# Column-tile weight splits traced at the highest priority in a four-mixer decoder layer

## The chip, the cores and the metric

The kernel runs on one core of a Trainium2 chip. A core has five engines with instruction queues of their own: TensorE (PE; its weight loads stand apart as PEld), VectorE (DVE), ScalarE (ACT), GpSimd (POOL) and SyncE (SP), which here only issues DMAs. Each engine takes its instructions in the order in which the built program holds them and waits on semaphores for data of the others. The metric is the time of one execution in microseconds of device time. A median over several runs is compared; 0.2% (2.5 us) is about the smallest difference that can be told from none.

## The reference, cut to what matters

One residual layer on x of 1024 tokens by 1024 channels, in float32. A normalised input goes through one combined projection; its columns feed four token mixers (A gated DeltaNet, B spatial gating, C RWKV-7, D native sparse attention) and the merge gates:

```python
h = rmsnorm(x, norm_gain)
proj = h @ w_in
ys = (gated_deltanet(...), spatial_gating(...), rwkv7_time_mix(...), native_sparse_attention(...))
gates = jnp.split(jax.nn.sigmoid(merge), N_MIXERS, axis=-1)
mixed = gates[0] * (ys[0] @ w_branch[0])
for i in range(1, N_MIXERS):
    mixed = mixed + gates[i] * (ys[i] @ w_branch[i])
return x + mixed @ w_out          # and a final rmsnorm
```

## The kernel before, in words

**Products in two halves.** To keep float32 accuracy each matrix is held as a high part (a rounded copy) and a low part (the remainder): `hh` and `hl` for the input, `wh` and `wl` for weights, and one product is three matmuls, `wh*hh`, `wl*hh` and `wh*hl`.

**Column tiles.** `col_tile` makes 128 columns of the projection for all 1024 tokens. It loads its weights in two halves (`load_w`, SP queue, tile `wt`, 3 buffers), splits each half (`split_w`: a cast on ScalarE makes `wh`, a subtraction on VectorE makes `wl`, 3 buffers each), and runs 48 matmuls of 128x512 (L1017 to L1019): 24 into one PSUM bank for the first 512 tokens, 24 into another for the second. The bank (`st`, 2 of them) is emptied by ScalarE into `stg` and stored to DRAM. With three buffers of `wh` and `wl`, one and a half tiles of split weights fit ahead of TensorE. There are 59 such tiles, 2832 matmuls. Three of the projection's tiles are made apart at the start, while the input is being normalised (L1111).

**The mixers.** `rwkv`, `gdn`, `nsa` and `gmlp` are traced one after the other, and their columns before each. Their work is small matmuls and long chains between TensorE, ScalarE and VectorE: in `rwkv` and `gdn` a triangular inverse of 16 steps on VectorE (`unit_lower_inverse`, L98 and L100), and a state that goes through chunks (L301 to L329, L550 to L578). The 32 column tiles of the merge gates are traced last, after `gmlp`.

**What sets the order.** Tile code is traced into a list of instructions, and at build time a list scheduler lays down the order of each engine: among the instructions that are ready in its own model of the machine, it takes the one with the highest priority, which without further words is the one traced earliest. So the column tiles traced after a mixer are the mixer's filler: their matmuls, casts and subtractions stand wherever the mixer's own instructions leave an engine free in that model. Once built, the order is fixed.

**After the mixers.** The outputs of the mixers are read back (`yr`, 16 loads of 256 KB through 2 buffers, L1230) and split into `yh` and `yl` (L1231, L1232); the pool that holds them opens when `gmlp` has ended. Then come the branch products (L1250 to L1252) and the output projection (L1281 to L1284).

Of the kernel before, what the change touches and what calls it, by code (L numbers as in the profile page):

```python
# [68 lines left out]
def bank(G, name="m", bufs=2):  # L69
    return G.ps.tile([128, 512], F32, name=name, bufs=bufs)  # L70
# [910 lines left out]
def body(tc, xT, x, w, wsm, rw_up, rw_cols, gd_conv, gd_hp, gd_gw, gm_ws, gm_bs, gm_lg, gm_lb,  # L981
# [3 lines left out]
    nc = tc.nc  # L985
    with ExitStack() as ctx:
# [10 lines left out]
        def load_w(src, k0, n):  # L997
            wt = sp.tile([128, 4, 128], F32, name="wt", bufs=3)
            nc.sync.dma_start(wt[:, :, :n], src[:, k0:k0 + 4])
            return wt  # L1000

        def split_w(wt, eng=nc.gpsimd, pool=sp, bufs=3):
            wh = pool.tile([128, 4, 128], F32R, name="wh", bufs=bufs)
            nc.scalar.copy(wh, wt)  # L1004
            wl = pool.tile([128, 4, 128], F32R, name="wl", bufs=bufs)
            eng.tensor_sub(wl, wt, wh.bitcast(F32))  # L1006
            return wh, wl

        def col_tile(c, evac):
            parts = [split_w(load_w(w[c], 4 * kh, 128), nc.vector) for kh in range(2)]  # L1010
            for th in range(2):
                sl = slice(512 * th, 512 * th + 512)
                p = bank(G, "st", 2)
                for k in range(8):
                    wh, wl = parts[k // 4]
                    kk = k % 4
                    nc.tensor.matmul(p, wh[:, kk], hh[:, k, sl], start=(k == 0), stop=False)  # L1017
                    nc.tensor.matmul(p, wl[:, kk], hh[:, k, sl], start=False, stop=False)  # L1018
                    nc.tensor.matmul(p, wh[:, kk], hl[:, k, sl], start=False, stop=(k == 7))  # L1019
                evac(p, sl)  # L1020
# [145 lines left out]
        for i in (0, 1, 4, 5):  # L1166
            col_tile(C_RW + i, park(rwd[i]))
        for i in range(2):
            col_tile(C_RWZ + i, park_silu(Z[2][i]))
# [21 lines left out]
        for i in (2, 3, 0, 1, 4, 5):  # L1191
            col_tile(C_GD + i, park(gdd[i]))
# [174 lines left out]
```

## Time and profile before

| | |
|---|---|
| median of three runs | 1254.97 us (1254.69 to 1255.78) |
| the profiled execution | 1258.43 us, of which 1256.7 us from the first to the last instruction |
| TensorE busy | 1185.8 us (94%) in 6214 matmul records |
| VectorE, ScalarE, GpSimd busy | 849.0 us (68%), 519.6 us (41%), 175.2 us (14%) |
| mean granted TensorE clock | 0.977 of full speed |

A busy time is that of the engine's records put together. Matmul records overlap, since one is issued while the last still drains, so a busy TensorE is not one that issues as fast as it can. A matmul of full float32 (transposes and the mixers' small products) leaves two records, one of the column tiles leaves one. The time outside the span (1.7 us) is not in the trace.

### The profile page before, as it was taken

How to read it: one execution, taken by the hardware profiler on the slowest of the kernel's cores; microseconds unless marked ns; L12 is line 12 of the kernel's file. 1: busy time of each engine (PE TensorE's matmuls, PEld its weight loads, DVE VectorE, ACT ScalarE, POOL GpSimd, SP SyncE). 2: the span in 40 equal slices, each digit the busy share in tenths (PEclk: the TensorE clock that was granted, in tenths of full speed). 3: DMA queues.
4: the chain of work that ended last, by engine and by line, in shares of the span. 5: the costliest groups of instructions: out<-in, count | busy, mean ns of one | idle time of the engine just before them, and what ended most of it. 6: DMA issues, size and time to landing. Idle time of an engine off the chain costs nothing. (4 is left out here: it accounts for less than half of the span.)

```text
span 1256.7 us, 17997 instructions
## 1 busy us (share of the span) xinstructions
PE 1185.8 (94%) x6214; PEld 962.6 (77%) x6214; DVE 849.0 (68%) x2181; ACT 519.6 (41%) x1302; POOL 175.2 (14%) x158
## 2 busy tenths in 40 slices
PE   6999999898999997998999999999999799999997
PEld 6987777786777785776777778787877577888886
DVE  6612697878774677878795579989876833588222
ACT  5422553361433355363533355645555343221212
POOL 4320000000002000010100000000000320576510
PEclk9999999998999998999999999999999999999999
DMA  5222453122211444212322422121114275676323
GB/s 196 101 93 101 134 149 103 45 70 67 98 59 59 112 149 121 98 61 81 115 75 85 162 94 76 64 76 56 59 47 145 100 238 186 214 236 217 110 84 126
DMA packets 113103, 140.09 MB, mean 111 GB/s; under 512 B 36544, under 2 KB 59968, under 8 KB 112884
## 3 DMA queue, kind: packets, MB, share of 16 engines
q1 hardware_dynamic: 95588, 107.22, 27.2%
q10 hardware_dynamic: 17424, 31.73, 6.6%
q8 instruction: 49, 0.80, 0.3%
q14 instruction: 42, 0.34, 0.1%
HBM read 94.78 MB, written 44.12 MB: 111 GB/s over the span
## 5 line engine op out<-in xcount | busy, mean ns | idle before, releaser
L1018 PE MATMUL st<-hh,wl 128*128 128x512 f32 x944 | 384.5, 407 | 9.4 <-DVE wl L1006 9.4
L1017 PE MATMUL st<-hh,wh 128*128 128x512 f32 x944 | 381.9, 406 | 3.2 <-ACT stg L1045 2.0
L1019 PE MATMUL st<-hl,wh 128*128 128x512 f32 x944 | 381.3, 404 | 0.0
L1018 PEld LDWEIGHTS st<-hh,wl 128*128 128x128 f32 x944 | 180.8, 192 | 44.0 <-DVE wl L1006 10.9
L1017 PEld LDWEIGHTS st<-hh,wh 128*128 128x128 f32 x944 | 180.2, 191 | 38.0 <-ACT stg L1045 3.5
L1019 PEld LDWEIGHTS st<-hl,wh 128*128 128x128 f32 x944 | 180.9, 192 | 32.3 <-issue 0.8
L1006 DVE TENSOR_TENSOR wl<-wt,wh 128x512 fp32r<-128x512 f32 x134 | 99.3, 744 | 94.2 <-ACT wh L1004 91.7
L1004 ACT CAST wh<-wt 128x512 fp32r<-128x512 f32 x140 | 86.4, 619 | 80.8 <-PE st L1019 66.5
L1045 ACT ACTIVATE stg<-st 128x512 f32<-128x512 f32 x64 | 38.2, 596 | 77.3 <-PE st L1019 76.9
L98 DVE TENSOR_TENSOR invP<-invX,invL 128x32 f32<-128x32 f32 (+15 forms) x128 | 55.7, 435 | 1.7
L100 DVE TENSOR_REDUCE invX<-invP 128x16 f32<-128x32 f32 (+15 forms) x128 | 54.9, 429 | 1.8
L915 ACT ACTIVATE P<-sc,m 128x512 f32<-128x512 f32 (+3 forms) x80 | 44.7, 564 | 25.3 <-DVE m L913 11.6
L1281 PE MATMUL sc<-woh,hh 128*128 128x512 f32 x128 | 49.8, 389 | 0.0
L1282 PE MATMUL sc<-wol,hh 128*128 128x512 f32 x128 | 49.8, 389 | 0.0
L1287 DVE TENSOR_TENSOR o<-sc,xr 128x512 f32<-128x512 f32 x16 | 11.1, 691 | 56.1 <-PE sc L1284 56.1
L1028 ACT COPY stg<-st 128x512 f32<-128x512 f32 x39 | 23.1, 591 | 61.0 <-PE st L1019 57.6
L1258 POOL TENSOR_TENSOR mx<-mx,stg 128x512 f32<-128x512 f32 x28 | 38.6, 1379 | 47.7 <-DVE stg L1257 46.6
L910 DVE TENSOR_REDUCE m<-sc 128x1 f32<-128x512 f32 (+3 forms) x80 | 40.7, 528 | 0.9 <-PE sc L835 0.3
L1264 ACT CAST hh<-mx 128x512 fp32r<-128x512 f32 x16 | 9.9, 621 | 62.6 <-POOL mx L1258 54.8
L30 POOL IOTA tril<- 128x128 f32 x1 | 0.2, 248 | 237.4 <-PE sc L835 237.4
L588 POOL TENSOR_TENSOR gst<-gst,mhalf 128x8 f32<-128x8 f32 x4 | 6.7, 1678 | 190.6 <-DVE gst L587 190.6
L254 POOL MEMSET sv<- 64x512 f32 x8 | 4.2, 519 | 207.8 <-ACT O L292 165.3
(457 smaller groups left out, 2400.7 us busy)
## 6 DMA issues: line engine op xcount, KB each, us to landing
wt<-in_w_dram SPq DMA_DIRECT2D x124, 256.0 KB, 2.7
gate<-stg ACTq DMA_DIRECT2D x64, 256.0 KB, 2.1
gt<-gate SPq DMA_DIRECT2D x32, 256.0 KB, 3.4
stg<-gate SPq DMA_DIRECT2D x32, 256.0 KB, 3.0
xt<-in_xT_dram SPq DMA_DIRECT2D x8, 512.0 KB, 5.0
wot<-in_wo_dram SPq DMA_DIRECT2D x16, 256.0 KB, 3.7
wt<-in_wb_dram SPq DMA_DIRECT2D x16, 256.0 KB, 3.5
xr<-in_x_dram SPq DMA_DIRECT2D x16, 256.0 KB, 2.5
```

The source lines that it names most:

```text
L98: nc.vector.tensor_mul(prv[:, :, :, :m], X[:, :, None, c:].to_broadcast([128, 8, 2, m]), L[:, None, c:c + 2, c:].to_broadcast([128, 8, 2, m]))
L100: nc.vector.tensor_reduce(X[:, :, c:c + 2], prv[:, :, :, :m], axis=AX.X, op=OP.add)
L910: nc.vector.tensor_reduce(m2[:, h, gi:gi + 1], pz[:, :n], axis=AX.X, op=OP.max, negate=True)
L915: nc.scalar.activation(Pt[gi][:, h, :n], pp[gi][:, :n], AF.Exp, bias=m2[:, h, 0:1], accum_out=ss[:, gi, h:h + 1])
L1004: nc.scalar.copy(wh, wt)
L1006: eng.tensor_sub(wl, wt, wh.bitcast(F32))
L1017: nc.tensor.matmul(p, wh[:, kk], hh[:, k, sl], start=(k == 0), stop=False)
L1018: nc.tensor.matmul(p, wl[:, kk], hh[:, k, sl], start=False, stop=False)
L1019: nc.tensor.matmul(p, wh[:, kk], hl[:, k, sl], start=False, stop=(k == 7))
L1258: (nc.vector if j == 7 else nc.gpsimd).tensor_add(mx, mx, g)
L1281: nc.tensor.matmul(p, mh[:, k, ts], a[:, k], start=(k == 0), stop=False)
L1282: nc.tensor.matmul(p, mh[:, k, ts], b[:, k], start=False, stop=False)
```

## The change

Of a column tile, the two instructions of each weight split are traced inside a block of highest priority. Nothing is computed otherwise, and no instruction, buffer or transfer is added; the load and the 48 matmuls keep the priority of their place. The splits of the three first tiles, of the branch weights and of the output weights stay as they were. Lines behind L1010 move by 4.

```diff
         def col_tile(c, evac):
-            parts = [split_w(load_w(w[c], 4 * kh, 128), nc.vector) for kh in range(2)]
+            parts = []
+            for kh in range(2):
+                wt = load_w(w[c], 4 * kh, 128)
+                with tc.high_priority():
+                    parts.append(split_w(wt, nc.vector))
             for th in range(2):
```

The built order differs on TensorE, VectorE, ScalarE and SP (on POOL it is the same). Three places are shown.

VectorE in `gdn`, the first quarter's inverse (`invP`, `invX`, L98 and L100, with 2 more columns at each step) beside the convolution of a later quarter (`cvt`, L465). Before, late in the inverse:

```order
L465 SCALAR_TENSOR_TENSOR cvt<-graw,cw,cvt 128x256
L100 TENSOR_REDUCE invX<-invP 128x8x2
L1038 SCALAR_TENSOR_TENSOR stg<-stg 128x512
L98 TENSOR_TENSOR invP<-invX,invL 128x16x26
L1038 SCALAR_TENSOR_TENSOR stg<-stg 128x512
L100 TENSOR_REDUCE invX<-invP 128x8x2
L480 SCALAR_TENSOR_TENSOR cvt<-gth,cvt 128x512
L98 TENSOR_TENSOR invP<-invX,invL 128x16x28
L1006 TENSOR_TENSOR wl<-wt,wh 128x512
L100 TENSOR_REDUCE invX<-invP 128x8x2
L1006 TENSOR_TENSOR wl<-wt,wh 128x512
```

Now, in the middle of the same inverse:

```order
L100 TENSOR_REDUCE invX<-invP 128x8x2
L1006 TENSOR_TENSOR wl<-wt,wh 128x512
L98 TENSOR_TENSOR invP<-invX,invL 128x16x12
L465 SCALAR_TENSOR_TENSOR cvt<-graw,cw,cvt 128x256
L100 TENSOR_REDUCE invX<-invP 128x8x2
L465 SCALAR_TENSOR_TENSOR cvt<-graw,cw,cvt 128x256
L98 TENSOR_TENSOR invP<-invX,invL 128x16x14
L465 SCALAR_TENSOR_TENSOR cvt<-graw,cw,cvt 128x256
L100 TENSOR_REDUCE invX<-invP 128x8x2
L1006 TENSOR_TENSOR wl<-wt,wh 128x512
L98 TENSOR_TENSOR invP<-invX,invL 128x16x16
```

Three splits stood together at the inverse's end; five now lie spread over it. By buffer number, the first of the three stood 61 rows behind the start of this inverse (L92) and now stands 10 rows ahead of it.

TensorE in `gdn`, one chunk of the state's chain (L560, L542, L544, L572, L576; rows of L1017 to L1019, now L1021 to L1023, are column tiles). Before:

```order
L576 MATMUL sc<-gSA_3540,gTB 128x128
L1019 MATMUL st<-hl,wh 128x512
L1017 MATMUL st<-hh,wh 128x512
L560 MATMUL sc<-gS,KQ_3536 128x128
L542 MATMUL sc<-gS,KQ_3536 128x128
L544 MATMUL sc<-gSA_3540,gKK 128x128
L572 MATMUL sc<-gR,gXT_3538 128x64
L576 MATMUL sc<-gSA_3539,gTB 128x128
```

Now, from L542 of the same chunk on:

```order
L542 MATMUL sc<-gS,KQ_3536 128x128
L544 MATMUL sc<-gSA_3540,gKK 128x128
L1023 MATMUL st<-hl,wh 128x512
L1021 MATMUL st<-hh,wh 128x512
L1022 MATMUL st<-hh,wl 128x512
L572 MATMUL sc<-gR,gXT_3538 128x64
L1023 MATMUL st<-hl,wh 128x512
L1021 MATMUL st<-hh,wh 128x512
L1022 MATMUL st<-hh,wl 128x512
L1023 MATMUL st<-hl,wh 128x512
L1021 MATMUL st<-hh,wh 128x512
L576 MATMUL sc<-gSA_3539,gTB 128x128
```

Where two column-tile matmuls stood between one L576 and the next, thirteen stand now (five of them ahead of L560).

SP's DMA issues after `gmlp`: loads of mixer outputs (`yr`), of output weights (`wot`), of parked gates (`gt`), and of weights into `wt`, either a column tile's (`in_w_dram`) or a branch product's (`in_wb_dram`). Before:

```order
L1230 DMA yr<-y__101 128x512
L999 DMA wt<-in_w_dram 128x512
L1230 DMA yr<-y__101 128x512
L1217 DMA wot<-in_wo_dram 128x512 x2
L1245 DMA gt<-gate_136 128x512
L1230 DMA yr<-y__101 128x512 x2
L1217 DMA wot<-in_wo_dram 128x512 x2
L999 DMA wt<-in_w_dram 128x512
L1230 DMA yr<-y__104 128x512
```

Now:

```order
L999 DMA wt<-in_wb_dram 128x512 x2
L1234 DMA yr<-y__101 128x512 x2
L1221 DMA wot<-in_wo_dram 128x512 x2
L1249 DMA gt<-gate_120 128x512
L1234 DMA yr<-y__101 128x512 x2
L1221 DMA wot<-in_wo_dram 128x512 x2
L999 DMA wt<-in_wb_dram 128x512
L1234 DMA yr<-y__104 128x512 x2
L999 DMA wt<-in_wb_dram 128x512
L1234 DMA yr<-y__104 128x512 x2
L1234 DMA yr<-y__102 128x512 x2
```

All loads of column weights now stand ahead of the first `yr`. On TensorE, 286 matmuls of column tiles stood behind `gmlp`'s last product (L681), in one piece up to the first branch product; now 155 do.

## Rows read from the trace of the kernel before

**Rows 1.** The page: span, and busy time by engine.
```profile
span 1256.7 us, 17997 instructions
PE 1185.8 (94%) x6214; PEld 962.6 (77%) x6214; DVE 849.0 (68%) x2181; ACT 519.6 (41%) x1302; POOL 175.2 (14%) x158
```

**Rows 2.** Busy time by stretch (start:end, length, then each engine), clock, DMA.
```profile
128.00:200.00 72.00, 70.93 (x392) 56.24 (x391) 62.97 (x148) 34.71 (x76) 0.00 (x0) 1.00 0.46 143
200.00:420.00 220.00, 205.79 (x1152) 168.85 (x1151) 155.19 (x464) 85.08 (x257) 15.79 (x19) 0.96 0.24 71
420.00:560.00 140.00, 127.01 (x638) 99.59 (x637) 107.97 (x303) 68.28 (x221) 6.28 (x4) 0.94 0.35 106
560.00:730.00 170.00, 157.98 (x942) 125.71 (x941) 123.32 (x365) 69.64 (x188) 9.65 (x10) 0.98 0.32 103
730.00:950.00 220.00, 217.16 (x1133) 174.82 (x1132) 189.40 (x570) 124.47 (x311) 0.25 (x1) 0.99 0.20 67
950.00:1006.00 56.00, 47.90 (x266) 37.86 (x264) 42.11 (x63) 22.05 (x33) 11.34 (x4) 0.96 0.38 129
```

**Rows 3.** TensorE's instructions in order of time: start, length, engine, line.
```profile
1046.17 0.39 PE L1017 MATMUL st<-hh,wh 128*128 128x512 f32 x1
...
1053.44 0.39 PE L1019 MATMUL st<-hl,wh 128*128 128x512 f32 x1
```

**Rows 4.** Waits of TensorE, 128 to 1006 us: total, times, longest.
```profile
PE st L1018 <- DVE wl L1006: 9.1, 2, 7.6
PE m L272 <- DVE AR L251: 7.0, 3, 3.6
PE m L681 <- DVE gmv L674: 4.7, 1, 4.7
PE m L488 <- DVE KQ L478: 4.4, 3, 2.1
PE sc L322 <- ACT XT L110: 3.3, 3, 2.1
PE sc L572 <- ACT gXT L110: 2.5, 2, 2.4
PE m L412 <- DVE w L407: 2.2, 1, 2.2
PE sc L120 <- DVE sqo L342: 2.1, 1, 2.1
```

**Rows 5.** Order of time around a late split, on ScalarE, VectorE, TensorE.
```profile
482.02 0.63 ACT L1004 CAST wh<-wt 128x512 fp32r<-128x512 f32 x1
...
500.13 0.68 DVE L1006 TENSOR_TENSOR wl<-wt,wh 128x512 fp32r<-128x512 f32 x1
500.74 0.60 DVE L100 TENSOR_REDUCE invX<-invP 128x16 f32<-128x448 f32 x1
...
500.87 0.80 PE L1018 MATMUL st<-hh,wl 128*128 128x512 f32 x1 [7.65 <-DVE wl L1006]
...
501.46 0.63 PE L1019 MATMUL st<-hl,wh 128*128 128x512 f32 x1
...
501.89 0.63 PE L1017 MATMUL st<-hh,wh 128*128 128x512 f32 x1
```

**Rows 6.** Busy time in three short stretches; columns as in rows 2.
```profile
583.00:588.00 5.00, 2.51 (x15) 1.76 (x15) 4.65 (x19) 2.78 (x4) 0.00 (x0) 1.00 0.00 0
484.00:508.00 24.00, 15.41 (x58) 12.01 (x57) 22.19 (x55) 6.32 (x11) 0.00 (x0) 0.79 0.42 126
292.00:304.00 12.00, 7.65 (x33) 6.38 (x31) 10.05 (x20) 0.99 (x2) 0.36 (x1) 0.76 0.19 56
```

**Rows 7.** Order of time: gmlp's end, last yr splits, first branch product.
```profile
1006.29 0.80 PE L1018 MATMUL st<-hh,wl 128*128 128x512 f32 x1
...
1048.25 0.69 DVE L1232 TENSOR_TENSOR yl<-yr,yh 128x512 fp32r<-128x512 f32 x1 [0.79 <-ACT yh L1231]
...
1053.09 0.69 DVE L1232 TENSOR_TENSOR yl<-yr,yh 128x512 fp32r<-128x512 f32 x1 [2.06 <-ACT yh L1231]
...
1075.50 0.39 PE L1250 MATMUL sc<-yh,wh 128*128 128x512 f32 x1
```

**Rows 8.** The casts' line L1004, 128 to 1006 us: what ScalarE stood idle for.
```profile
L1004 ACT CAST wh<-wt x94: 604/620/642, 138.7 to 997.3; 128x512 fp32r<-128x512 f32 x94
its engine sat idle before it (us, times) until:
  PE st L1019: 50.5, 29
```

## The prediction

> **What bounds the kernel now.** I read the page first, then busy time by stretch, then TensorE's waits, then the order of time around the longest of them. The page says that TensorE is busy 1185.8 of 1256.7 us [rows 1]; where nothing holds it up it issues a column-tile matmul every (1053.44 - 1046.17)/32 = 0.227 us [rows 3]. Nearly all work on it is fixed, so the question is where it stands idle. Busy time by stretch answers: between 128 and 1006 us, while the mixers run, the idle time is 1.1 + 14.2 + 13.0 + 12.0 + 2.8 + 8.1 = 51 us [rows 2]. It lies in `rwkv` (200 to 420), `gdn` (420 to 730) and `gmlp` (950 to 1006), hardly in `nsa`. VectorE is busy 70 to 77% of those first three stretches, so in their dense parts it is the limit and TensorE lives on filler.
>
> The waits say whom it waits for: mostly VectorE's mixer results, and once, for 7.6 us, a weight split [rows 4]. In that case the cast was done at 482.7, but the subtraction ran only at 500.13, since VectorE took the inverse and the convolution first; TensorE had nothing else in its order and stood 7.65 us. Then it issued at 0.43 us (501.46, 501.89) instead of 0.227 [rows 5]: the granted clock of 484 to 508 is 0.79 [rows 6], so part of that stretch ran at 1.2 instead of 2.4 GHz.
>
> **The change, part by part.** No instruction is added. A split costs VectorE about 0.61 us (500.13 to 500.74 [rows 5]) and ScalarE 0.62 [rows 8], before as after. What moves is their place, and with it the column-tile matmuls: 286 stood behind `gmlp`'s last product, 155 do now. So 131 matmuls, 131 x 0.227 = 29.7 us of TensorE's time, go ahead of that product. TensorE does the same work, hence the time falls by just as much idle time as they fill. Between nothing (they land where it was busy anyway) and 29.7 us, I go from place to place, comparing the matmuls counted in the order with the wait there.
>
> First, ahead of `rwkv`'s products L272 at 295 us, 37 stand instead of 20: 17 x 0.227 = 3.9, enough for the wait of 3.6 [rows 4]; the stretch around it had 12 - 7.65 = 4.35 us idle [rows 6]. I take 3.6.
> Second, the late split: 70 instead of 55 stand ahead of the inverse's transposes, 15 x 0.227 = 3.4 us. I take this and not the 7.65, because VectorE was busy 22.19 of 24 us there [rows 6] and its list, not the split, sets when the inverse ends.
> Third, the `gdn` chunk at 583: 11 more matmuls are 2.5 us, and 5 - 2.51 = 2.5 us were idle [rows 6]. I take 2.5.
> Fourth, L488: its waits sum to 4.4 us, the longest 2.1 [rows 4]; two of the places get 7 and 9 matmuls more (1.6 and 2.0 us). I take 3.0.
> Fifth, smaller ones: the other waits for `AR` (3.4 us left, 6 more matmuls, 1.4), for `gXT` (2.4 us, 9 more, 2.0), for `sqo` (2.1 us, 5 more, 1.1), and the second wait for a `wl` (1.5) [rows 4]: 6.0 together.
> Left as they are: `gmv` (4.7 us; 4 matmuls instead of 3) and `w` (2.2 us; 73 instead of 79).
> Sum: 3.6 + 3.4 + 2.5 + 3.0 + 6.0 = 18.5 us.
>
> Against it stand two costs. **At the start**, three splits now lie among the first scalings of the input by its norm (L1104, L1106), which TensorE soon needs: 3 x 0.61 = 1.8 us, nothing at best. **Behind the mixers**, the 286 matmuls covered the reading of the mixers' outputs. It began with `gmlp`'s end; the splits that the second branch product needs were done at 1048.94 and 1053.78, 42.7 and 47.5 us after TensorE took up the filler at 1006.29 [rows 7]. The first branch product came at 1075.50, 69.2 us after; less the 131 matmuls moved that would be 39.5. But by 47.5 us only 24 branch matmuls (5.4 us) can be through, which amounts to a start at 42.1: 2.6 us lost. Bounds: 0, if `yr` loads go faster now that no column weights stand between them on SP's queue, and 47.5 - 39.5 = 8.0 if none of the branch work gets ahead.
>
> The granted clock is a term that I leave at nothing. In the three stretches of rows 2 with most idle time it is 0.96, 0.94 and 0.98: at most 0.04 x 220 + 0.06 x 140 + 0.02 x 170 = 20.6 us. The late split alone gives perhaps 2 us back (11 matmuls at 0.43). New waits of the same order will come from a reshuffled order, and I set the two against each other.
> The Trainium skill (TensorE: Matmul & The Clock Gate, "HAM oscillation — how this bites in real kernels") has it that TensorE falls back to half speed after idling and that half of the throttled time is lost; the 0.43 us behind the 7.65 us wait agree. If that held for every wait closed here, a further 10 us or so, half of the 20.6, would come back: that is the second rival below.
>
> Net: -18.5 + 1.8 + 2.6 = -14.1 us. The profiled execution took 1258.43, so the same one would take 1244.3. The median of the runs is 3.5 us lower, 1254.97; the forecast is 1254.97 - 14.1 = 1241.
>
> **The rivals.**
> *Slower: casts that hold up ScalarE.* A cast waits until TensorE has let go of one of three `wh` buffers. In 29 of 94 casts ScalarE stood idle for that, 50.5 us, 1.74 each [rows 8]. That cost little as long as the casts stood behind the mixers' own copies. At the highest priority a cast is put where the scheduler's model sees the buffer free; if the chip is behind the model there, the state copies queued behind it wait too, and TensorE for them. Eight such waits (14.1/1.74) on the chain eat the gain, fourteen give 1254.97 - 14.1 + 24.4 = 1265. For it speak the 65 casts that had no such wait so far; against it that in `rwkv` and `gdn` ScalarE is busy under half of the time [rows 2].
> The Trainium skill (TensorE: Matmul & The Clock Gate, the table at its head, "Engine queue depth") calls the queues of ScalarE and VectorE strictly first in, first out, which is what makes this rival possible; the 50.5 us agree.
> *More: nearly all 131 fill idle time.* 51 us are there. Then -29.7 + 1.8 + 2.6 = -25.3, 1230 us; with the clock's 10 us 1220.
> *A wash: VectorE is the limit nearly everywhere.* Then only the `gdn` chunk, `sqo`, the second `wl` and half of the late split count, 2.5 + 1.1 + 1.5 + 1.7 = 6.8, against 1.8 and between 2.6 and 8.0: -2.4 to +3.0, 1253 to 1258.
>
> **How the numbers follow.** A measurement of this kernel tells 0.2%, 2.5 us, from no change. Chances: the forecast 0.53 (its own range 1232 to 1249), more 0.15, a wash 0.13 (0.02 faster, 0.09 within 2.5 us, 0.02 slower), slower 0.19. Faster is 0.53 + 0.15 + 0.02 = 0.70, same 0.09, slower 0.21. Below 1222 lies about a third of "more" and above 1264 half of "slower" (0.05 + 0.10), so 1222 to 1264 leaves out less than 2 in 10.
>
> **What would show it.** Right: the 7.6 us wait of L1018 for `wl` gone; TensorE's idle time in 200 to 730 down from 39 us to below 28; the chunk at 583 without its gap; behind `gmlp`'s last product some 35 us of filler, then a new wait of a branch product for `yl` of at most 8 us; VectorE's and ScalarE's busy totals unchanged. Wrong, and how: more idle time on ScalarE ahead of L1004 together with longer waits of TensorE for ScalarE's copies (`gSA`, `R`, `sv`) would be the first rival; TensorE waits that only move to other VectorE results, with `gmlp` ending about 29 us later than before, the wash. The forecast fails most easily in the fillings, which are counted one by one in an order that is reshuffled throughout.

## The result, and the profile after

The changed kernel takes 1235.17 us (median of 5 runs, 1233.39 to 1235.81). In the same comparison the kernel before took 1255.78 us (5 runs, 1254.69 to 1257.62): a ratio of 0.9832, 95% interval 0.9818 to 0.9845, or 20.6 us less. The forecast was 1241, with 70 in 100 for faster. The profiled execution took 1235.68 us, span 1233.9 against 1256.7, 22.8 us less; the kernel before was profiled in an execution 2.7 us above its median, so the two profiles differ by more than the medians do.

The page's busy totals, to be read beside [rows 1]:

```profile
span 1233.9 us, 18017 instructions
PE 1174.9 (95%) x6214; PEld 952.2 (77%) x6214; DVE 849.0 (69%) x2181; ACT 523.2 (42%) x1302; POOL 175.6 (14%) x158
```

VectorE's total is the same and ScalarE's 3.6 us higher, so the work is the same. TensorE's busy time fell by 10.9 us with as many records: the same matmuls took less time each, a first sign that part of the gain is clock. Busy time by stretch, as in [rows 2]:

```profile
128.00:200.00 72.00, 70.97 (x396) 56.45 (x395) 62.74 (x147) 34.75 (x76) 0.00 (x0) 1.00 0.47 146
200.00:420.00 220.00, 211.23 (x1206) 174.23 (x1205) 157.25 (x466) 89.52 (x263) 15.60 (x19) 0.99 0.25 75
420.00:560.00 140.00, 127.86 (x644) 100.79 (x643) 108.41 (x301) 66.26 (x207) 5.91 (x4) 0.95 0.36 112
560.00:730.00 170.00, 164.09 (x987) 129.73 (x986) 125.83 (x373) 75.08 (x207) 9.80 (x10) 1.00 0.33 106
730.00:950.00 220.00, 215.74 (x1119) 172.74 (x1120) 188.28 (x562) 124.26 (x306) 0.25 (x1) 1.00 0.21 67
950.00:1006.00 56.00, 50.41 (x273) 40.09 (x273) 41.31 (x65) 22.82 (x34) 12.38 (x4) 0.98 0.39 131
```

TensorE's idle time in 200 to 730 is 8.8 + 12.1 + 5.9 = 26.8 us (39.2 before), in 128 to 1006 altogether 37.7 (51.2). The clock is higher in every one of these stretches in which it was below 1.00. The three short stretches of [rows 6]:

```profile
583.00:588.00 5.00, 5.00 (x28) 4.09 (x28) 4.75 (x16) 0.77 (x3) 0.00 (x0) 1.00 0.74 205
484.00:508.00 24.00, 17.33 (x75) 14.21 (x76) 23.07 (x57) 7.38 (x12) 0.69 (x1) 0.88 0.27 79
292.00:304.00 12.00, 10.57 (x59) 8.07 (x58) 10.42 (x24) 1.60 (x4) 1.71 (x1) 1.00 0.21 78
```

The first has no idle time left, the third 1.4 us instead of 4.35 and its clock back at 1.00. The middle one still has 6.7 us idle. Its clock looks better (0.88, before 0.79) only because the stretch ends at 508; taken to 516 it is the same in both kernels, before and after:

```profile
484.00:516.00 32.00, 23.30 (x97) 18.27 (x95) 27.09 (x68) 10.42 (x22) 0.00 (x0) 0.84 0.36 111
```
```profile
484.00:516.00 32.00, 25.33 (x103) 20.50 (x104) 25.69 (x66) 10.65 (x23) 0.69 (x1) 0.84 0.38 121
```

TensorE's waits, 128 to 1006 us, beside [rows 4]:

```profile
PE sc L103 <- DVE invX L100: 8.2, 2, 6.7
PE m L681 <- DVE gmv L674: 3.5, 2, 1.9
PE sc L572 <- ACT gXT L110: 3.2, 3, 2.0
...
PE m L488 <- DVE KQ L478: 2.8, 4, 2.1
PE m L272 <- DVE AR L251: 2.3, 2, 2.0
```

The wait for `wl` is gone. In its place TensorE waits 6.7 us at 500 to 507 us for the inverse itself. Behind the mixers, TensorE in order of time, which answers to [rows 7]:

```profile
1009.58 1.57 PE L681 MATMUL m<-gmw,gmv 128*64 128x128 f32 x16
...
1046.35 0.39 PE L1254 MATMUL sc<-yh,wh 128*128 128x512 f32 x1
...
1051.08 0.50 PE L1254 MATMUL st<-yh,wh 128*128 128x512 f32 x1 [3.21 <-ACT yh L1235]
...
1058.03 0.50 PE L1254 MATMUL st<-yh,wh 128*128 128x512 f32 x1 [0.82 <-ACT yh L1235]
```

The last `gmlp` product starts at 1010.9 (the last of the 16 in the first row), 4.9 us later than before although 29.7 us of column matmuls were moved ahead of it. The first branch product follows 35.5 us later (69.6 before), and then waits for the mixers' outputs. ScalarE ahead of the casts, 128 to 1006 us, beside [rows 8]:

```profile
L1004 ACT CAST wh<-wt x98: 602/621/641, 136.6 to 993.1; 128x512 fp32r<-128x512 f32 x98
...
its engine sat idle before it (us, times) until:
  PE st L1023: 77.9, 59
```

### The profile page after: what moved, and what is told of

Same layout as the page of the kernel before. It is cut to its first block, busy times and chain, and to the rows that moved or that the text cites. A ratio compares the mean times of both kernels' runs of the same rounds, so it can differ in the third digit from the quotient of the medians.

```text
span 1233.9 us, 18017 instructions
## 1 busy us (share of the span) xinstructions
PE 1174.9 (95%) x6214; PEld 952.2 (77%) x6214; DVE 849.0 (69%) x2181; ACT 523.2 (42%) x1302; POOL 175.6 (14%) x158
## 5 line engine op out<-in xcount | busy, mean ns | idle before, releaser
L1021 PE MATMUL st<-hh,wh 128*128 128x512 f32 x944 | 381.2, 404 | 0.0
L1023 PE MATMUL st<-hl,wh 128*128 128x512 f32 x944 | 380.6, 403 | 0.0
L1022 PE MATMUL st<-hh,wl 128*128 128x512 f32 x944 | 380.1, 403 | 0.0
L1023 PEld LDWEIGHTS st<-hl,wh 128*128 128x128 f32 x944 | 179.3, 190 | 32.7 <-issue 1.3
L1021 PEld LDWEIGHTS st<-hh,wh 128*128 128x128 f32 x944 | 179.3, 190 | 31.6 <-issue 0.9
L1004 ACT CAST wh<-wt 128x512 fp32r<-128x512 f32 x140 | 86.5, 618 | 131.0 <-PE st L1023 117.7
L98 DVE TENSOR_TENSOR invP<-invX,invL 128x32 f32<-128x32 f32 (+15 forms) x128 | 55.8, 436 | 1.4
L100 DVE TENSOR_REDUCE invX<-invP 128x16 f32<-128x32 f32 (+15 forms) x128 | 55.2, 431 | 1.8
L910 DVE TENSOR_REDUCE m<-sc 128x1 f32<-128x384 f32 (+3 forms) x80 | 41.0, 531 | 1.4 <-PE sc L835 0.9
L1032 ACT COPY stg<-st 128x512 f32<-128x512 f32 x39 | 22.8, 585 | 43.9 <-PE st L1023 41.1
```

Source lines behind the costliest of these rows:

```text
L98: nc.vector.tensor_mul(prv[:, :, :, :m], X[:, :, None, c:].to_broadcast([128, 8, 2, m]), L[:, None, c:c + 2, c:].to_broadcast([128, 8, 2, m]))
L100: nc.vector.tensor_reduce(X[:, :, c:c + 2], prv[:, :, :, :m], axis=AX.X, op=OP.add)
L910: nc.vector.tensor_reduce(m2[:, h, gi:gi + 1], pz[:, :n], axis=AX.X, op=OP.max, negate=True)
```

## The experiments

Times are medians against the kernel before on the same chip, whose median was 1255.8 for the first four kernels, 1255.5 for the next and 1255.9 for the last; a single run is called so. For the ten kernels with an account below I read the same numbers from each trace: how many column-tile matmuls stand behind `gmlp`'s last product, when that product starts, and between 46.4 us and then TensorE's idle time and the time in which it was busy at the lower clock (1.2 instead of 2.4 GHz), half of which I count as lost.

**The cast alone.**

```diff
-                with tc.high_priority():
-                    parts.append(split_w(wt, nc.vector))
+                wh = sp.tile([128, 4, 128], F32R, name="wh", bufs=3)
+                with tc.high_priority():
+                    nc.scalar.copy(wh, wt)
+                wl = sp.tile([128, 4, 128], F32R, name="wl", bufs=3)
+                nc.vector.tensor_sub(wl, wt, wh.bitcast(F32))
+                parts.append((wh, wl))
```

> Theory (the subtraction's place on VectorE moves column-tile matmuls ahead of gmlp's last product, and about 0.19 us comes back for each, 24.8 us for 131): with the cast alone at the highest priority 291 matmuls stand behind that product instead of 286, so nothing is gained: within 0.2% of the kernel before, some 1255 us, and the 7.6 us wait for the late split is still there. Rival A (the cast, waiting on ScalarE behind the mixers' copies, was what came late): most of the gain is here, 1235 to 1240 us. Rival B (any reshuffled order would have gained): some per cent either way.

1248.48 us (1246.74 to 1249.90), ratio 0.9943 (0.9927 to 0.9958): 7.3 us gained where the theory had nothing and rival A 15 to 20. No matmul was moved ahead, and the split still comes late:

```profile
PE st L1026 <- DVE wl L1017: 8.4, 3, 5.0
```

Idle time fell by 1.9 us only, but time busy at the lower clock from 40.4 to 30.3 us. The theory, which had made the gain a matter of matmuls moved, is short of one term. Of the 8.1 us that this kernel regains in the account below, 5.0 come from the clock and 1.9 from idle time, so rival B, that a reshuffled order by itself gains or loses, is not excluded for these 7 us.

**The subtraction alone.** `tc.high_priority()` stands around `nc.vector.tensor_sub` instead.

> Theory: the subtraction alone at the highest priority leaves 121 matmuls behind gmlp's last product (155 with both), 165 moved. Up to there at most 165 x 0.19 = 31 us are regained, less if the idle time is used up. But 121 x 0.227 = 27.5 us of filler no longer cover the reading of the mixers' outputs, which in the changed kernel was done some 42 us after gmlp's end (35.4 us of filler and 6.5 us of new waits): about 14 us lost at the branch products. Net -31 + 14 = -17: 1238 us, between 1234 and 1245. Rival A (the cast is needed): about 1255. Rival C (the filler behind the mixers costs nothing to lose): 1255 - 31 = 1224.

1244.10 us (1241.19 to 1245.56), ratio 0.9904 (0.9887 to 0.9921). 29.4 us are regained up to `gmlp`'s end, and from the first branch product to the first output product it takes 103.5 us instead of 87.0. So the subtraction's place is enough to move the work, and the filler behind the mixers has a value: rival A and rival C fall.

**The merge gates' tiles alone**, and **the filler of `rwkv` alone**.

```diff
-                with tc.high_priority():
+                with tc.high_priority() if c >= C_MG else nullcontext():
```
```diff
-                with tc.high_priority():
+                with tc.high_priority() if C_GD <= c < C_NK else nullcontext():
```

> Only the merge gates' tiles (the 32 last) get the change; the order up to the inverse at 500 us stays as before, with its late split. Theory: 220 matmuls behind gmlp's last product instead of 286, 66 moved, 66 x 0.19 = 12.5 us, nothing lost at the end (220 x 0.227 = 50 us cover the reading): 1243 us, and the 7.6 us wait of TensorE for wl is still in the trace. Rival D (the late split and the clock behind it are the bulk of the gain): no more than 5 us gained, 1250 us or above.

> Only the tiles of gdn's columns (the filler of rwkv) get the change. Theory: 339 matmuls stand behind gmlp's last product instead of 286, 53 more, so TensorE idles more among the mixers: 53 x 0.19 = 10 us slower, 1265 us, although these splits themselves come earlier. Rival E (a split that comes earlier helps wherever it is): faster than before, 1245 to 1252 us.

The first: 1247.15 us (1243.46 to 1247.83), ratio 0.9925 (0.9907 to 0.9942), 8.7 us gained (12.5 expected) with the late split in place:

```profile
PE st L1022 <- DVE wl L1006: 7.1, 1, 7.1
```

So 8.7 us come without the late split. That it is not the bulk of the rest either is seen in the changed kernel, where its wait of 7.65 us has become one of 6.67 at the same place, with the same clock from 484 to 516. The second: 1257.28 us (1251.72 to 1262.88, 12 runs), ratio 0.9999 (0.9984 to 1.0013). That is neither 10 us slower nor faster. With 53 more matmuls behind it, `gmlp`'s last product came 10.3 us earlier; they are worth 12.0, so only 1.7 us were lost in the profiled run, not 10. A fixed price per matmul moved does not hold. The spread is telling: over the 12 runs of this one program the time follows the mean granted clock, from 1262.88 us at 0.975 to 1251.72 at 0.984.

**More buffers for the outputs' reading**, in the changed kernel and with the subtraction alone.

```diff
-                            yr = M.tile([128, 512], F32, name="yr", bufs=2)
+                            yr = M.tile([128, 512], F32, name="yr", bufs=4)
```

> The changed kernel with 4 instead of 2 buffers for yr. Theory: behind gmlp the branch products wait for the mixers' outputs (6.4 us more between the first branch and the first output product than before the change), because 16 loads of 3.7 us each go through 2 buffers, one each 2.4 us from 1020.6 to 1058.0. With 4 buffers the last split comes more than 10 us earlier and the wait goes: 6 us faster than the changed kernel, about 1229 us. Rival (ScalarE's and VectorE's splits or the DMA queue set that pace): 1235 us, with the wait unchanged.

> The subtraction alone at the highest priority, with 4 buffers for yr. In the kernel with the subtraction alone the branch stretch took 103.5 us instead of 87.0: 16.5 us lost to the outputs' reading, which 121 matmuls of filler no longer cover. Theory: most of that comes back, 10 to 16 us of its 1244.1: 1228 to 1234 us, as fast as the changed kernel or faster. Rival (buffers don't set the pace): 1244 us.

The first: 1229.74 us (1228.99 to 1235.16), ratio 0.9811 (0.9785 to 0.9838), where 1229 was expected. The 16 casts into `yh`, in the changed kernel and then with 4 buffers:

```profile
L1235 ACT CAST yh<-yr x16: 617/621/623, 1020.6 to 1058.0; 128x512 fp32r<-128x512 f32 x16
```
```profile
L1235 ACT CAST yh<-yr x16: 610/621/625, 1019.4 to 1039.9; 128x512 fp32r<-128x512 f32 x16
```

The last one comes 18 us earlier, and the branch stretch falls from 93.4 to 88.7 us. These 4.7 us are what the traces show; the medians are 5.4 us apart, but the ratios' intervals overlap with the change's, and two of the five runs took 1233.9 and 1235.2 us. The second: 1234.90 us (1233.51 to 1236.37), just past the 1234 expected; 9.2 us came back. What was left of its wait is another one:

```profile
PE sc L1258 <- ACT wh L1004: 4.6, 1, 4.6
```

That is the cast of a branch product's weights, which on ScalarE comes behind the last casts into `yh` and behind a cast of output weights that itself waited 2.58 us for its load.

**Whole tiles at the highest priority.** `col_tile` is traced inside `tc.high_priority()`, matmuls and all.

> Whole column tiles, with their matmuls, at the highest priority, so that no column-tile matmul stands behind gmlp's last product and most of the 2832 stand ahead of gdn. Theory (filler is worth something only where TensorE would wait): the mixers' chains lie bare afterwards, and the time grows by more than 100 us, to 1350 us or above. Rival (the earlier the column tiles, the better): faster than 1235 us.

1731.48 us in a single run. TensorE and its clock in 40 slices of the span:

```profile
PE   7999999999999999999463256445466676249998
...
PEclk9999999999999999999555556555566677569999
```

With the filler used up in the first half, TensorE is busy about half of the time in the mixers and runs most of it at the lower clock. "The earlier the better" falls.

**Four buffers of split weights, no priority.**

```diff
-        def split_w(wt, eng=nc.gpsimd, pool=sp, bufs=3):
+        def split_w(wt, eng=nc.gpsimd, pool=sp, bufs=4):
```

> The kernel before, without any raised priority, with 4 instead of 3 buffers of wh and wl. 226 instead of 286 matmuls stand behind gmlp's last product: 60 moved. Theory: 60 x 0.19 = 11 us regained, and nothing lost behind gmlp, since 226 x 0.227 = 51 us cover the reading of some 42 us: 1244 us. Of this between a third and a half is the granted clock, which in the median of the runs is 0.979 before and 0.989 in the changed kernel, so here about 0.983 to 0.985. Rival (only the priority itself, which puts splits ahead of the mixers' VectorE work, makes the gain): no faster than before, 1255 us.

1227.21 us (1226.97 to 1232.69), ratio 0.9787 (0.9763 to 0.9812): 28 us gained, 17 more than expected, and better than the change itself (0.9818 to 0.9845). So priority is one way to the gain and not the only one. Its waits:

```profile
PE sc L103 <- DVE invX L100: 12.3, 3, 8.0
...
PE st L1018 <- DVE wl L1006: 3.5, 1, 3.5
```

It keeps long waits, but few: 6 over 2 us up to `gmlp`'s end, as against 9 before.

**The price of a wait by itself.** From the first output product to the end TensorE has no idle time, and every trace so far shows 87.2 us for it. There, in the kernel before, waits are put in: the result of a group is turned into zeros by a chain on VectorE, and the next groups add a product with them. `at` is (2, 6, 10) with n = 10, or 1 to 9 with n = 1; the fill is there in the second kernel only.

```diff
+                        if zr is not None:
+                            nc.tensor.matmul(p, zr[:, 0:128], zr, start=True, stop=False)
...
+                        if 8 * half + t in at:
+                            zc = FP.tile([128, 512], F32, name="zc")
+                            nc.vector.tensor_scalar(zc, p, 0.0, 0.0, op0=OP.mult, op1=OP.mult)
+                            for _ in range(n):
+                                nc.vector.tensor_sub(zc, zc, zc)
+                            zr = FP.tile([128, 512], F32R, name="zr")
+                            nc.scalar.copy(zr, zc)
+                            d = sbank(G)
+                            for k in range(36):
+                                nc.tensor.matmul(d, mh[:, k % 8, ts], a[:, k % 8], start=(k == 0), stop=(k == 35))
```

> The clock's price by itself, in the kernel before. From the first output product to the end TensorE has no idle time and takes 87.2 us in every trace so far. Here three waits are put into that stretch: behind three of the 16 groups VectorE turns the group's result into zeros in a chain of 11 instructions, about 8.5 us, and the next group first adds a product with these zeros (13 more matmuls, 3.0 us). No other group is ready meanwhile. Theory (a long wait costs more than itself, since the granted clock is half for 3.4 to 10.2 us behind it): 87.2 + 3.0 + 25.5 + 5 to 15 = 121 to 131 us from the first output product to the end. Rival (a wait costs itself and no more): 116 us.

> The same three waits, with 36 matmuls whose result nobody reads in each of them (36 x 0.227 = 8.2 us), so that TensorE is busy while the zeros are made. Theory: the granted clock stays at full speed, and the stretch takes 87.2 + 3.0 + 25.5 = 116 us, 5 to 15 less than with bare waits although TensorE does 108 matmuls more. Rival (the clock is no matter of these waits): the same time as with bare waits.

> Nine short waits instead of three long ones in the same stretch: behind nine groups in a row a chain of 2 VectorE instructions and a cast, about 2.4 us, 22 us in all; 14 more matmuls, 3.2 us. Theory (what costs clock is the length of a wait, not the idle time in all, which is why a reshuffled order with shorter waits was faster with the same idle time): 87.2 + 3.2 + 22 = 112 us, granted clock close to 1. Rival (clock goes with idle time): 117 to 125 us, granted clock below 0.95.

Single runs of 1302.07, 1298.54 and 1304.46 us; what counts is the stretch. TensorE's wait for the zeros (total, times, longest) and the stretch's busy time and clock, for the three long waits:

```profile
PE sc L1282 <- ACT zr L1294: 33.5, 3, 12.9
```
```profile
1162.86:1293.38 130.52, 97.06 (x398) 78.38 (x396) 46.56 (x67) 22.90 (x49) 26.22 (x23) 0.86 0.20 73
```

for the same waits filled:

```profile
PE sc L1282 <- ACT zr L1294: 9.1, 3, 4.9
```
```profile
1161.38:1289.82 128.44, 119.33 (x506) 97.04 (x504) 46.70 (x67) 22.93 (x49) 26.75 (x23) 0.96 0.21 74
```

and for the nine short ones:

```profile
PE sc L1282 <- ACT zr L1294: 25.1, 9, 3.1
```
```profile
1163.57:1295.73 132.16, 107.10 (x399) 84.07 (x397) 30.61 (x52) 26.05 (x55) 24.22 (x23) 0.88 0.20 72
```

The chains took longer than planned, 10.2 to 12.9 us a long wait, so 36 matmuls did not fill them; still the filled stretch ended 2.1 us sooner than the bare one, with 24.5 us more work in it. The account of each single run, with its measured waits: long, 87.2 + 3.0 + 33.5 = 123.7 us, measured 130.5, 6.8 more for three waits. Filled, 87.2 + 3.0 + 24.5 (108 matmuls) + 9.1 = 123.8, measured 128.4, 4.6 more. Short, 87.2 + 3.2 + 25.1 = 115.5, measured 132.2, 16.7 more for nine waits. Here a wait thus costs itself and some 2 us besides: 6.8/3 = 2.3 us if it is 10 to 13 us long, 16.7/9 = 1.9 if it is 2.6 to 3.1. What these us are, TensorE behind one short wait:

```profile
1187.60 0.50 PE L1282 MATMUL sc<-zr 128*128 128x512 f32 x1 [2.77 <-ACT zr L1294]
...
1188.28 0.63 PE L1285 MATMUL sc<-wol,hh 128*128 128x512 f32 x1
1188.71 0.63 PE L1284 MATMUL sc<-woh,hh 128*128 128x512 f32 x1
...
1191.57 0.40 PE L1285 MATMUL sc<-wol,hh 128*128 128x512 f32 x1
1191.81 0.40 PE L1284 MATMUL sc<-woh,hh 128*128 128x512 f32 x1
```

0.43 us from one matmul to the next for a while behind the wait, then 0.23 to 0.24 again: the two levels of the clock. My theory that only long waits cost clock falls, since nine of nine short ones did, and so does the rival that clock goes with idle time (33.5 us idle cost 6.8, 25.1 idle cost 16.7). In these runs it goes by the number of waits.

That is no rule for every wait. The nine stand 10.2 to 10.6 us apart in like surroundings, so they are one case repeated and not nine independent ones. Behind the second of the filled waits, 2.1 us long, the clock stayed at full speed (1.00 from 1224 to 1240), and in the kernel with four split buffers it did so around waits of 3.49 and 2.84 us:

```profile
492.63 0.50 PE L1018 MATMUL st<-hh,wl 128*128 128x512 f32 x1 [3.49 <-DVE wl L1006]
...
498.75 0.44 PE L103 MATMUL sc<-ident,invX 128*128 128x128 f32 x2 [2.84 <-DVE invX L100]
```
```profile
484.00:506.00 22.00, 15.67 (x70) 12.25 (x68) 17.93 (x40) 8.01 (x17) 0.00 (x0) 1.00 0.49 157
```

In the kernel before, it stayed at full speed behind waits of 2.10 us (ending at 367.1) and 2.15 us (at 602.7), but fell to half behind waits of 1.99 us (at 553.3) and 1.87 us (at 587.4). So the length of a wait alone does not decide whether it costs clock, and what does is not shown here.

The Trainium skill (TensorE: Matmul & The Clock Gate, "HAM oscillation — how this bites in real kernels") has it that half of the throttled time is lost. TensorE was busy at the lower clock for 29.9 us of the stretch with nine waits, half of it 14.9 of the 16.7 us, which agrees; with the three long waits it was 12.5 us, half of it 6.3 of the 6.8.

**Four buffers and the merge gates' priority together**, with 4 `yr` buffers.

> Four buffers of wh and wl and of yr, and the highest priority for the splits of the merge gates' 32 tiles alone: 203 matmuls stand behind gmlp's last product (226 with four buffers alone, 155 in the changed kernel). Theory: 23 more matmuls ahead of it than with four buffers, 23 x 0.19 = 4 us less than 1227, and with four yr buffers 203 x 0.227 = 46 us still cover the reading of the outputs: 1223 us, between 1219 and 1228. Rival (four buffers have already closed what can be closed): 1227 us or above.

1231.58 us (1227.86 to 1233.66), ratio 0.9813 (0.9790 to 0.9837). The rival's outcome: no faster than four buffers alone, and not to be told from them (their intervals overlap). Its six runs follow the clock, 1227.86 us at 0.993 and 1233.06 and 1233.66 at 0.986, where the four-buffer kernel's five lie between 1226.97 at 0.991 and 1232.69 at 0.988.

**The account.** Regained is (1005.9 - start of the last `gmlp` product) + 0.227 x (286 - matmuls behind it). The two columns after it are counted in the trace: idle time less than before, and half of the time busy at the lower clock less than before (51.2 and 40.4 us before). "Behind" is what lies between that product and the first output product beyond 0.227 us for each of the matmuls there and 87.0 for the branch products (4.7 us before).

| kernel | matmuls behind | last product | regained | from idle | from clock | behind |
|---|---|---|---|---|---|---|
| the change | 155 | 1010.9 | 24.8 | 13.5 | 10.7 | 6.7 |
| cast alone | 291 | 996.7 | 8.1 | 1.9 | 5.0 | 1.8 |
| subtraction alone | 121 | 1014.0 | 29.4 | 16.6 | 13.4 | 16.9 |
| merge gates alone | 220 | 1006.6 | 14.4 | 6.7 | 9.1 | 4.1 |
| `rwkv`'s filler alone | 339 | 995.6 | -1.7 | -5.7 | 0.3 | 7.4 |
| change, 4 `yr` | 155 | 1009.3 | 26.4 | 13.3 | 12.4 | 2.4 |
| subtraction, 4 `yr` | 121 | 1015.0 | 28.4 | 16.7 | 11.8 | 9.6 |
| 4 split buffers | 226 | 995.7 | 23.8 | 9.3 | 10.4 | 2.7 |
| 4 buffers, merge gates | 203 | 998.6 | 26.2 | 8.5 | 16.6 | 0.2 |

In every row idle and clock together come within 4.1 us of what was regained; in six of the nine within 1.2. For the change, 24.8 regained less 2.0 more behind are the 22.8 us between the two spans. Each row is one profiled run, though, and runs of one program differ in their clock: the profile of `rwkv`'s filler is the slowest of its 12 runs, that of four split buffers the slowest of its 5 (5.5 us above the median), that of four buffers with the merge gates the fastest of its 6. So differences of a few us between two rows, in the clock's column above all, are not shown to be the kernels' own.

## Why the prediction came out as it did

**The direction and the way were right.** The matmuls moved ahead of `gmlp`'s end filled idle time on TensorE and the wait for the late split went. The subtraction's place does it alone; the cast's place alone moves no matmul ahead, and what it gains is mostly clock.

**The size: the fillings.** Of 18.5 us forecast, 13.5 came. The waits for `AR` fell by 4.7 us (3.6 + 1.4 forecast) and the chunk at 583 gave its 2.5. The late split was forecast at 3.4, because VectorE's list and not the split sets when the inverse ends; that is what happened, only more so: 9.1 us of waits for `wl` became 8.2 of waits for the inverse. At L488 the wait for `KQ` fell by 1.6 of the 3.0 forecast, but 1.8 us of waits for ScalarE's copies `gjk` and `gTB` came up there, so L488 gave nothing. `sqo` gave 0.4 of 1.1, and the waits for `gXT` grew by 0.7 instead of falling by 2.0. `gmv`, left as it was, gave 1.2.

**The step that failed: the granted clock, left at nothing.** I set the clock given back against "new waits of the same order" from a reshuffled order. They did not come: waits over 2 us up to `gmlp`'s end fell from 9 to 4, and the time busy at the lower clock from 40.4 to 19.0 us, worth 10.7. The runs of the comparisons say the same by another road: the median granted clock was 0.979 for the kernel before (17 runs) and 0.989 for the changed one (5 runs). Within the runs of one program 0.001 of clock goes with 0.81 us (a line through 52 runs of six kernels, those before and after and the first four experiments, each kernel about its own mean), so 0.010 are some 8 us. The bound of 20.6 was about right (half of 40.4 is 20.2). The second rival's "10 us or so" was the term's right size by luck, since it was reached by halving a bound. What changed in the trace: up to `gmlp`'s end ten stretches at the lower clock became four. Of the ten, seven begin during or just behind a wait of over 2 us and three by a shorter one; of the four, two each. The late split's place kept its stretch. Why some waits are followed by half clock and others not, the runs leave open.

**The costs.** At the start 1.8 us were forecast and nothing was lost: the first column tile starts at 46.45 us, before at 46.43. Behind the mixers 2.6 were forecast, 2.0 came (6.7 less 4.7), as a wait of the branch products for the outputs, at most 3.2 us long; the rows named `yh` where I had named `yl`. That it was the two `yr` buffers that set this pace is shown by four.

**What was luck.** The fillings were 5.0 us too high. That hid part of the 10.7 us of clock and the 2.4 us of costs that the forecast missed the other way, so 1241 lay nearer to the measured 1235 than its terms deserved.

**The rival on the other side.** ScalarE's casts do stand idle for a `wh` buffer more often, 59 times and 77.9 us instead of 29 times and 50.5 [rows 8]. It cost little to be seen: TensorE's waits for `gXT` grew by 0.7 us and those for `gjk` and `gTB` came up (1.8), but the one for `gSA` (1.9 before) went, those for `XT` fell from 3.3 to 1.6, and none for `R` or `sv` came up.

**Open.** Why four buffers alone regain as much with 60 matmuls moved as the change does with 131 is only partly told by the account, which leaves 4.1 us there without a name; and why one order has fewer waits than another was not derived from anything but its trace.

## What to carry to other kernels

On an engine whose clock falls when it waits, read the granted clock behind the waits as well as the idle time: in a stretch without other idle time each wait put in cost about 2 us beyond its own length, and nine short ones cost more than three long ones with more idle time in all. Not every wait costs that, so look for it in the trace and don't take it from the number or length of the waits. When filler is taken from behind a stage, ask what it covered there and widen that first: with 4 buffers for the outputs' reading the changed kernel's branch stretch was 4.7 us shorter. And try depth beside priority: one more buffer for the split weights gained 28 us by itself.

## What was not expected of the hardware

Nine waits of 2.6 to 3.1 us each left the clock at half behind them, every one, and cost 16.7 us together, more than twice what three of 10 to 13 us cost; yet in another kernel waits of 3.49 and 2.84 us left it at full speed. And one program's time can move by 11 us along with the clock that it is granted: 1251.72 to 1262.88 us, at 0.984 and 0.975.
